# A hybrid encoder layer on one core: turned tiles by way of DRAM, a bound on close short products, and new planner estimates

## The chip, the cores and the metric

The kernel runs on one core of one Trainium2 chip. The metric is the time of one execution in device microseconds (us), given as the median of several runs. The kernel before takes 1050.35 us (median of three runs, 1049.75 to 1050.82).

The core has five engines that run on their own and meet at semaphores: TensorE (PE in the profile, with its weight loads as PEld), VectorE (DVE), ScalarE (ACT), GpSimd (POOL) and SyncE (SP), which here does nothing but issue transfers.

## The reference

One layer over 512 frames of width 2048, all in float32. A wide projection gives the inputs of two mixers that both read the same x; their gated outputs are joined and projected back.

```python
proj = jnp.einsum('btd,dc->btc', h, w_in[l])              # 512 x 2048 by 2048 x 8320
rw = _token_shift(proj[..., :RWKV_COLS], shift_mu[l])
hg = proj[..., RWKV_COLS:]
o_rwkv, v_first = _rwkv7_branch(rw, ...)                  # 16 heads of 64
o_hgrn = _hgrn2_branch(hg, lower_bounds[l], g_norm_w[l])  # 8 heads of 128
y = jnp.einsum('btc,cd->btd', jnp.concatenate([o_rwkv, o_hgrn], -1), w_out[l])
h = _layer_norm(ALPHA * h + y, ln_w[l], ln_b[l])
```

The first mixer steps a 64 x 64 state for each head through time:

```python
sa = jnp.einsum('bhij,bhj->bhi', S, a_t)
S = S * w_t[:, :, None, :] + sa[..., None] * b_t[:, :, None, :] + v_t[..., None] * k_t[:, :, None, :]
out = jnp.einsum('bhij,bhj->bhi', S, r_t)
```

The second is a gated linear recurrence with a decay for each channel, in its chunkwise form.

## The kernel before, in words

**The large products.** Each float32 operand is split into a high and a low part of a faster type (`split`: one ACT copy, `wh`, and one DVE subtraction, `wl`), and three products of 128 x 128 by 512 columns stand for one exact product (`three`, line 457; in the first units line 1205). There are 65 column units of 128 in the input projection and 16 row and column blocks in the output projection, each with 16 steps over the inner dimension. Weights arrive as 512 KB tiles `wr`.

**The mixers are fed in between.** Both mixers are written as Python generators that yield single operations, and a planner (class `Plan`) places them between the large products while the program is written. It keeps a clock for each engine, advances it by an estimated cost for each operation, and after every large product it asks the threads (`pump`, `step`): an operation is put into its engine's instruction stream if by these clocks its inputs are there about now, else its thread waits. `LEAD`, `SLACK` and `EARLY` say how near is near enough. The hardware then runs each engine's stream strictly in order, and semaphores, not the planner, hold an instruction back. A wrong estimate changes no result, but it puts an instruction where it waits, with everything behind it on its engine.

**Short products.** The mixers need many products of blocks smaller than 128 x 128: mode `"narrow"`, all written by `mm` (line 329). They come in series, which the planner holds until about all of a series can run: 32 by 16 or 32 columns (`blocks32`), 32 x 32 inverses (`quarters` of `rwkv_invert`), 64 x 64 blocks (`folded`, `outputs`), 64 x 128 scores (`rwkv_prep`). A float32 product of this kind is two matmul records and two weight loads in the profile.

**Turned tiles.** Three tiles are needed transposed over all 128 partitions: `bk` (eight times, 512 KB), the values `z` (eight times, 256 KB) and the keys of six of the heads of the second mixer (192 KB). `turned` (line 402) does it in two steps: one DVE instruction transposes every 32 x 32 block in place (`dtr`), and then transfers from SBUF to SBUF put the blocks where they belong, 16 for `bk` and the keys and 8 for `z`, each 32 partitions by pieces of 128 bytes. The profile shows them as `q<-q`, `zz<-ksq` and `g<-ksq`, all issued by line 310 (`send`).

**Groups.** Heads go through in pairs: `rwkv_prep` makes operands and scores and then turns; `rwkv_invert` inverts; `folded` forms the products for the scan; `rwkv_scan` steps over the chunks; `outputs`, `rwkv_finish`; and for the other mixer `hgrn_heads` and `hgrn_out`. The reciprocal square roots of the norms are computed on POOL (`rsqrt`, line 384), and a DVE instruction multiplies by them.

**Buffers.** PSUM has four banks for large products (`main`) and four for the rest (`mix`). A `main` bank is emptied by `shift`, `gates` or `silu2` on ACT and DVE (lines 342, 343, 361). The split weight parts `wh`, `wl` have three buffers each.

Of the kernel before, what the change touches and what calls it, by code (L numbers as in the profile page):

```python
# [15 lines left out]
P = 128  # L16
T = 512
# [45 lines left out]
class Plan:  # L63
# [9 lines left out]
             ("whole", "narrow"): 0.1, ("narrow", "main"): 0.26, ("narrow", "whole"): 0.2}  # L73
    REST = 1.5
    LEAD = -0.35
    SLACK = 0.6
    EARLY = 0.5

    def __init__(self, room):
# [4 lines left out]
        self.ready, self.busy, self.banks = {}, {}, set()  # L84
        self.room = room
# [69 lines left out]
    def add(self, queue, gen):  # L155
        queue.append([gen, None, False])
# [4 lines left out]
    def step(self, th):  # L161

        now = self.clock["pe"]
        gen, item, held = th
        if not held:
# [4 lines left out]
            th[1:] = item, True  # L170
        if callable(item):
            if not item():
                return False
        else:
            way = self.best(item)
            end, s, r, e, f = way
            if e == "pe":
                if r > now + self.LEAD or not self.worth(item, now):
# [3 lines left out]
            self.issue(item, way)  # L182
        th[2] = False
# [58 lines left out]
def mixer_kernel(ctx, tc, head, x_r, w_all, par, up, ln_wb, consts, hmask, out):  # L242
# [53 lines left out]
    def landed(*tiles):  # L296
# [8 lines left out]

        return test
# [13 lines left out]
    def mm(o, l, r, start=True, stop=True, **kw):  # L320
# [61 lines left out]
    def rsqrt(o, i):  # L382
        return Op([("pool", 0.25 + size(o) * 0.19,
                    lambda: pool.tensor_tensor(o, i, mhalf[:, : size(o)], ALU.pow))], [i], [o])

    def memset(o, v):
        return Op([("pool", 0.1, lambda: pool.memset(o, v))], [], [o])
# [9 lines left out]
    def turned(dst, src, tmp, rows=4, base=0):  # L397


        name = dst.tensor.name  # L400
# [36 lines left out]
    whole_parts = set()  # L437

    def ready(i, home=None):

        if i < 2 * nload and i not in parts:
            parts[i] = home() if home else tuple(st(t, [P, QT], F32R) for t in ("wh", "wl"))

# [8 lines left out]
    def three(ps, lh, ll, rh, rl, first, last):  # L452
        n = size(rh)
        for i, (l, r) in enumerate(((lh, rh), (lh, rl), (ll, rh))):
            plan.clock["pe"] += n / 2400 + 0.0135 + plan.turn("main")
# [11 lines left out]
    def part(i, width):  # L467

        ready(i)
        hi, lo = parts[i]  # L470
# [155 lines left out]
    hc = [slice(64 * h, 64 * h + 64) for h in range(2)]  # L626

    def rwkv_prep(S, p):
# [75 lines left out]
        S["ar"], S["bk"] = ar, bk  # L704
# [39 lines left out]
        z = take("zz", [P, NCH, P])  # L744
        yield room(ksq=1)
        tmp = take("ksq")
        yield from turned(z, chunks(v), chunks(tmp), rows=2, base=64)
# [3 lines left out]
    def folded(SS, sc):  # L751
# [4 lines left out]
        yield landed(*zs, *bks, sc)  # L756
        pvs = [take("main") for _ in SS]
        pbs = [take("mix") for _ in SS]
        for half, (z, bk, pv, pb) in enumerate(zip(zs, bks, pvs, pbs)):
            for c in range(NCH):  # L760
                i, cs = half * 16 + 2 * c, slice(c * C, c * C + C)
                for h in range(2):
                    yield mm(pv[hc[h], cs], sc[64:128, 0, i + h], z[64:128, c, hc[h]])
                    yield mm(pb[hc[1 - h], cs], sc[0:64, 0, i + 1 - h], bk[0:64, c, hc[1 - h]])
        more = plan.free("mix", 2)
# [10 lines left out]
        if more:  # L776
            yield from beside()
# [902 lines left out]
```

## Time and profile before

| | |
|---|---|
| median of three runs | 1050.35 us (1049.75 to 1050.82) |
| the profiled execution's own time | 1049.71 us |
| its span, first to last instruction | 1047.9 us |
| granted TensorE clock, mean | 0.999 |
| PE busy | 1034.7 us (99%), 7708 matmul records |
| PEld busy | 857.5 us (82%) |
| DVE / ACT / POOL busy | 754.5 (72%) / 436.8 (42%) / 41.8 us (4%) |
| share of the 16 DMA engines | 37.1%, in 97 824 packets, most of them (67 120) under 512 bytes |

The span is cut off at the first and last instruction, so the execution's own time is 1.8 us longer than it. Ends of matmuls are modelled: a large product is shown as 393 ns long while the next one starts about 227 ns after it, so distances between starts say more than durations. In views of waits, "issue" is time in which the engine waited for nothing that the profile shows. In a timeline a row holds equal instructions that follow each other; its second number runs from the start of the first to the end of the last.

### The profile page before, as it was taken

The numbers are of one execution on the slowest core, as the hardware profiler recorded it, in microseconds if no ns is written. First come the engines' busy times: TensorE is split into PE (matmuls) and PEld (weight loads), VectorE is DVE, ScalarE is ACT, GpSimd is POOL, SyncE is SP. The second block draws the span as 40 slices with busy tenths as digits, with TensorE's granted clock in tenths as the row PEclk, the third lists the DMA queues.
The fourth block names the chain that finished last, engine by engine and source line by source line (L and its number), as shares of the span: only waits on it lengthen the run. The fifth ranks groups of instructions, "written<-read, shape, count | busy, mean of one in ns | idle before, by whom it ended". The sixth has DMA issues, their size and how long they took to land.

```text
span 1047.9 us, 19640 instructions
## 1 busy us (share of the span) xinstructions
PE 1034.7 (99%) x7708; PEld 857.5 (82%) x7708; DVE 754.5 (72%) x1599; ACT 436.8 (42%) x817; POOL 41.8 (4%) x77
## 2 busy tenths in 40 slices
PE   9999999999999999999999999999999999999997
PEld 7888888888888888878888788888888888888885
DVE  7474898767759988667689767775999886526456
ACT  6444434543443355353533364435335444223321
POOL 0000001001000010010000100100001011000000
PEclk9999999999999999999999999999999999999999
DMA  9135342133253432224443222344342245445613
GB/s 332 53 103 130 90 104 85 60 93 99 77 140 94 123 87 68 87 74 113 112 116 104 82 73 73 105 110 106 105 117 81 64 157 183 145 129 170 193 60 131
DMA packets 98061, 116.03 MB, mean 111 GB/s; under 512 B 67120, under 2 KB 68912, under 8 KB 97840
## 3 DMA queue, kind: packets, MB, share of 16 engines
q1 hardware_dynamic: 97824, 114.57, 37.1%
q8 instruction: 61, 1.00, 0.4%
q14 instruction: 32, 0.26, 0.1%
q10 hardware_dynamic: 144, 0.20, 0.1%
HBM read 99.92 MB, written 7.34 MB: 102 GB/s over the span
## 4 chain that ended last, share of the span: by engine, by line
PE 93%; DMA 2%; DVE 2%; SPq 1%; issue 1%; ACT 0%; POOL 0%; DVEq 0%
PE main L457 70%; PE mix L329 11%; PE mix L457 8%; PE main L1205 3%; DMA wr<-w_all 2%; PE main L329 1%; PE mix L333 1%; SPq L310 1%; DMA q<-head 0%; DVE t L352 0%; DVE wl L352 0%; DVE inv L361 0%; DMA g<-ksq 0%; ACT t L342 0%; DVE q L361 0%
## 5 line engine op out<-in xcount | busy, mean ns | idle before, releaser
L457 PE MATMUL main<-xh,wh 128*128 128x512 f32 x864 | 339.6, 393 | 1.9 <-DVE t L361 1.9
L457 PE MATMUL main<-xh,wl 128*128 128x512 f32 x864 | 341.2, 395 | 0.0
L457 PE MATMUL main<-xl,wh 128*128 128x512 f32 x864 | 339.7, 393 | 0.0
L342 ACT ACTIVATE wh<-wr 128x512 fp32r<-128x512 f32 x299 | 186.5, 627 | 244.7 <-PE main L457 193.6
L352 DVE TENSOR_TENSOR wl<-wr,wh 128x512 fp32r<-128x512 f32 x299 | 203.3, 682 | 75.1 <-ACT wh L342 73.6
L457 PEld LDWEIGHTS main<-xh,wh 128*128 128x128 f32 x864 | 162.4, 188 | 35.3 <-DVE t L361 2.3
L457 PEld LDWEIGHTS main<-xh,wl 128*128 128x128 f32 x864 | 162.4, 188 | 33.3 <-DVE wl L352 0.3
L457 PEld LDWEIGHTS main<-xl,wh 128*128 128x128 f32 x864 | 162.3, 188 | 33.2
L457 PE MATMUL main<-wl,xh 128*128 128x512 f32 (+1 forms) x262 | 102.2, 390 | 0.3 <-DVE wl L352 0.3
L457 PE MATMUL main<-wh,xh 128*128 128x512 f32 (+1 forms) x262 | 102.1, 390 | 0.0
L457 PE MATMUL main<-wh,xl 128*128 128x512 f32 (+1 forms) x262 | 101.8, 388 | 0.0
L457 PEld LDWEIGHTS main<-wl,xh 128*128 128x128 f32 x262 | 49.2, 188 | 10.3 <-DVE wl L352 0.6
L457 PEld LDWEIGHTS main<-wh,xh 128*128 128x128 f32 x262 | 49.2, 188 | 10.2 <-ACT wh L342 0.2
L457 PEld LDWEIGHTS main<-wh,xl 128*128 128x128 f32 x262 | 49.2, 188 | 9.8
L361 DVE SCALAR_TENSOR_TENSOR bd<-mix,pc,bd 64x64 f32<-64x64 f32 x112 | 31.7, 283 | 17.1 <-PE mix L329 15.0
L343 ACT ACTIVATE t<-main,om 128x512 f32<-128x512 f32 x33 | 22.2, 686 | 51.6 <-PE main L457 42.4
L342 ACT ACTIVATE t<-mix 64x128 f32<-64x128 f32 (+2 forms) x65 | 17.6, 272 | 56.6 <-PE mix L329 28.2
L352 DVE TENSOR_TENSOR inv<-inv 64x30 f32<-64x30 f32 (+14 forms) x120 | 38.5, 321 | 2.8
L352 DVE TENSOR_TENSOR inv<-inv,inv 64x30 f32<-64x30 f32 (+14 forms) x120 | 38.5, 321 | 2.7
L361 DVE SCALAR_TENSOR_TENSOR t<-main,pr,t 128x511 f32<-128x511 f32 x33 | 24.3, 745 | 19.7 <-ACT t L343 19.6
L352 DVE TENSOR_TENSOR t<-t,tot 128x256 f32<-128x256 f32 x96 | 37.5, 417 | 0.3
L343 ACT ACTIVATE t<-main 128x512 f32<-128x512 f32 x32 | 18.6, 595 | 32.5 <-PE main L457 32.3
(218 smaller groups left out, 1311.9 us busy)
## 6 DMA issues: line engine op xcount, KB each, us to landing
wr<-w_all SPq DMA_DIRECT2D x156, 512.0 KB, 3.7
q<-head SPq DMA_DIRECT2D x15, 448.0 KB, 6.1
q<-q SPq DMA_DIRECT2D x128, 32.0 KB, 2.7
g<-x_r SPq DMA_DIRECT2D x16, 256.0 KB, 4.0
spill<-g SPq DMA_DIRECT2D x12, 256.0 KB, 3.7
t<-spill SPq DMA_DIRECT2D x12, 256.0 KB, 4.3
out<-q SPq DMA_DIRECT2D x12, 256.0 KB, 2.5
zz<-ksq SPq DMA_DIRECT2D x64, 32.0 KB, 3.0
```

The costliest lines, as they stand in the source:

```text
L310: nc.sync.dma_start(o, i)
L329: return Op([("pe", cost, lambda: pe.matmul(o, l, r, start=start, stop=stop, **kw))], [l, r], [o], mode="narrow" if narrow else "main" if ...
L333: return Op([("pe", 0.11, lambda: pe.transpose(o, i, ident))], [i], [o])
L342: return "act", cost, lambda: sc_e.activation(o, i, f, scale=scale)
L343: return "act", cost, lambda: sc_e.activation(o, i, f, scale=scale, bias=bias)
L352: return dve_op([a, b], o, lambda: dve.tensor_tensor(o, a, b, f), base=0.16 if o.shape[0] < P and size(o) == C and o.tensor.name in tags e ...
L361: return dve_op([a, b], o, lambda: dve.scalar_tensor_tensor(o, a, s, b, f1, f2), per=0.00113, base=0.085 if o.shape[0] == P else 0.25 if s ...
L457: pe.matmul(ps, l, r, start=first and i == 0, stop=last and i == 2)
L1205: pe.matmul(pss[a], *ops, start=k == 0 and low == of == 0, stop=k == KT - 1 and low == 1)
```

## The change

There are three parts. Besides these, `z` is laid out in another order of its columns (four blocks of 32 first, then chunks), with the reads of it adapted.

**1. Turned tiles.** `turned` writes the tile, after the same 32 x 32 transposes, to a DRAM scratch tile `far` in one transfer, waits in the planner until its estimate says that it has landed, and loads it back in one transfer for each block of 32 rows (four for `bk` and the keys, two for `z`), in pieces of 1 KB (384 bytes for the keys). The order of blocks inside a partition is then not the one that the products need for `bk` and the keys, so one copy on ACT puts it right. The turning of `bk` and `z` becomes a thread of its own (`rwkv_turn`), so the preparation of the next head need not stand behind it.

**2. A bound.** A series of short products is started only if those of the last 3.0 us and the new ones together are at most 68 (`BURST`, `WITHIN`, `room_for`); each series says its length by `batch`. In `folded` the third series is always held apart.

**3. Estimates.** Costs of short products, of the way back from them, of `rsqrt` and `memset` on POOL and of the large products are new; transfers of turned tiles are taken as landed 4.0 us after their issue (2.6 before); and the planner now knows when the buffers `wh` and `wl` come free.

```diff
@@ class Plan
-             ("whole", "narrow"): 0.1, ("narrow", "main"): 0.26, ("narrow", "whole"): 0.2}
+             ("whole", "narrow"): 0.1, ("narrow", "main"): 0.11, ("narrow", "whole"): 0.1}
...
+    BURST, WITHIN = 68, 3.0
...
             if op.mode == "narrow":
                 self.rest = end + self.REST
+                self.short.append(end)
...
+    def room_for(self, n):
+
+        since = self.clock["pe"] - self.WITHIN
+        while self.short and self.short[0] < since:
+            self.short.pop(0)
+        return not self.short or len(self.short) + n <= self.BURST
...
@@ def step
         if callable(item):
             if not item():
                 return False
+            th[3] = getattr(item, "batch", th[3])
         else:
...
             if e == "pe":
+                if th[3] and item.mode == "narrow":
+                    if not self.room_for(th[3]):
+                        return False
...
+            if item.mode == "narrow":
+                th[3] = 0
@@ def mm
-        if r.dtype == F32R:
-            cost = n / 2400 + 0.0135
+        if cost:
+            pass
+        elif r.dtype == F32R:
+            cost = n / 2400 + 0.0145
         elif narrow:
-            cost = 0.025 if m <= 32 else 0.06 if m <= 64 else 0.16
+            cost = 0.0135 + n * 0.0002 if m <= 32 else 0.06 if m <= 64 else 0.115
@@ def rsqrt
-        return Op([("pool", 0.25 + size(o) * 0.19,
+        return Op([("pool", {1: 0.5, 4: 1.35, 8: 1.8}[size(o)],
@@ def turned
-        yield dtr(tmp, src)
+        far = dpool.tile([P, rows, size(tmp) // rows], F32, tag=nm("far"), name=nm("far"))
+        yield dtr(tmp.rearrange("p b c j -> p c b j"), src)
         yield lambda: by_now(tmp)
-        for a in range(4):
-            for b in range(rows):
-                yield lambda: plan.clock["sp"] <= plan.clock["pe"] + 0.2
-                o = base + 32 * b
-                send(dst[o : o + 32, :, 32 * a : 32 * a + 32],
-                     tmp[32 * a : 32 * a + 32, :, 32 * b : 32 * b + 32], 0.65)
-        plan.ready[name] = plan.busy[tmp.tensor.name] = (plan.clock["sp"] + 2.6, "dma")
+        yield lambda: plan.clock["sp"] <= plan.clock["pe"] + 0.2
+        send(far, tmp.rearrange("p b c j -> p b (c j)"))
+        there = plan.busy[tmp.tensor.name] = (plan.clock["sp"] + 4.0, "dma")
+        for b in range(rows):
+            yield lambda: there[0] <= plan.clock["pe"] and plan.clock["sp"] <= plan.clock["pe"] + 0.2
+            send(dst(b).rearrange("i a c j -> i a (c j)"), far[:, b].rearrange("(a i) x -> i a x", a=4))
+        plan.ready[dst(0).tensor.name] = (plan.clock["sp"] + 4.0, "dma")
@@ def ready, def part
+                ring.append(i)
+                before = ring[-1 - BUFS["wh"]] if len(ring) > BUFS["wh"] else -1
+                for t in parts[i]:
+                    plan.busy[t.tensor.name] = (over.get(before, 0.0), "pe")
...
+        for k in range(len(over), min(i, last_parts)):
+            over[k] = plan.clock["pe"]
@@ def rwkv_prep
-        yield landed(bk, ar)
-        yield room(mix=2, main=3)
-        pss = [take(tag) for tag in ("main", "mix") for h in range(2)]
+        yield landed(bk, ar, n=16)
+        yield lambda: plan.free("mix", 2) and plan.free("main", 3) or plan.free("mix", 4)
+        pss = [take(tag) for tag in ("main" if plan.free("main", 3) else "mix", "mix") for h in range(2)]
...
+        plan.add(turns, rwkv_turn(S, bk, r))
+
+    def rwkv_turn(S, bk, r):
         yield room(q4=1)
         tmp = take("q4", [P, NCH, P])
-        yield from turned(bk, bk, tmp)
-        drop(tmp)
+        bk4 = blocks(bk.rearrange("p c f -> p (c f)"), NCH)
+        yield from turned(lambda b: bk4[32 * b : 32 * b + 32], bk, blocks(tmp.rearrange("p c f -> p (c f)"), NCH))
+        yield act(tmp.rearrange("p c (a j) -> p c a j", j=32), bk4.rearrange("p a c j -> p c a j"), AF.Copy)
+        drop(bk)
+        S["bk"] = tmp
@@ def folded
-        yield landed(*zs, *bks, sc)
+        yield landed(*zs, *bks, sc, n=64)
...
-        if not more:
-            yield room(mix=2)
-            yield landed(sc)
-            yield from beside()
+        yield room(mix=2)
+        yield landed(sc, n=32)
+        yield from beside()
@@ def hgrn_out
-            yield from turned(kt, tiles(k)[:, 0:3], tiles(tmp)[:, 0:3])
+            g4 = blocks(g[:, : 3 * P], 3)
+            yield from turned(lambda b: g4[32 * b : 32 * b + 32], kt, blocks(tmp[:, : 3 * P], 3))
             drop(tmp)
+            yield act(kt.rearrange("p c (a j) -> p c a j", j=32), g4.rearrange("p a c j -> p c a j"), AF.Copy)
```

**How the instruction streams move.** The number of products on PE is the same. The first place is the first series of 64 x 64 products on PE (`folded`, for the first pair of heads). `mix` tiles with sources `t` belong to `hgrn_heads`, `zz` and `q` with `big` to `folded`; `main` with `xh`, `wh`, `wl` are large products. Before, 64 products of one and 64 of the other stand in one series:

```order
L457 MATMUL main_1850<-xl_85,wh_1654 128x512
L329 MATMUL mix_1847<-t_1049 32x16 x16
L329 MATMUL mix_1847<-t_1258 32x16 x16
L329 MATMUL mix_1847<-t_954,t_1050 32x16 x16
L329 MATMUL mix_1847<-t_1161,t_1259 32x16 x16
L329 MATMUL main_1924<-zz_872,big_694 64x64
L329 MATMUL mix_1926<-q_447,big_694 64x64
...
L329 MATMUL mix_1927<-q_933,big_694 64x64
L457 MATMUL main_1850<-xh_69,wl_1655 128x512
```

In the change the same products stand in two series, with many large products and another short series between them:

```order
L485 MATMUL main_1285<-wh_1679,xh_80 128x512
L348 MATMUL mix_1736<-t_1075 32x16 x16
L348 MATMUL mix_1736<-t_1272 32x16 x16
L348 MATMUL mix_1736<-t_961,t_1076 32x16 x16
L348 MATMUL mix_1736<-t_1173,t_1273 32x16 x16
L485 MATMUL main_1285<-wl_1680,xh_80 128x512
...
L485 MATMUL main_1955<-xh_69,wh_1884 128x512
L348 MATMUL main_1936<-zz_1000,big_694 64x64
L348 MATMUL mix_1938<-q_743,big_694 64x64
```

Over the whole stream there were 36 such unbroken series, and there are now 43; the longest was 128 products (five more had 96) and is now 64.

The second place is SP at the first turn of `bk` (`q_447`; `wr` are weights). Before:

```order
L310 DMA wr_751<-w_all 128x1024
L310 DMA q_447<-q_735 32x8x32 x6
L310 DMA wr_792<-w_all 128x1024
L310 DMA q_447<-q_735 32x8x32 x8
L310 DMA wr_834<-w_all 128x1024
L310 DMA q_447<-q_735 32x8x32 x2
L310 DMA wr_885<-w_all 128x1024
```

and in the change:

```order
L327 DMA wr_764<-w_all 128x1024
L327 DMA far_744<-q_743 128x1024
L327 DMA up_789<-up 128x256
L327 DMA q_447<-far_744 32x4x256
L327 DMA wr_813<-w_all 128x1024
L327 DMA q_447<-far_744 32x4x256 x3
L327 DMA wr_855<-w_all 128x1024
```

SP's transfers in all go from 530 to 336. The third place is DVE in `hgrn_out` of the third head, where `rs` holds the factors of a norm that POOL computes between the `TENSOR_SCALAR` and the product with `mix`, and the instruction after that product frees a `main` bank. Before:

```order
L365 TENSOR_REDUCE rs_4837<-t_3389 128x4
L358 TENSOR_SCALAR rs_4837<-rs_4837 128x4
L352 TENSOR_TENSOR wl_4846<-wr_4703,wh_4845 128x512
L352 TENSOR_TENSOR t_3389<-mix_4825,rs_4837 128x512
L361 SCALAR_TENSOR_TENSOR t_4859<-main_4212,pr,t_4859 128x511
```

and in the change, where other work has moved in before the `TENSOR_SCALAR`, while one `wl` still stands behind it:

```order
L384 TENSOR_REDUCE rs_4688<-t_3368 128x4
L371 TENSOR_TENSOR wl_4696<-wr_4545,wh_4695 128x512
L371 TENSOR_TENSOR t_3105<-t_3105,sm_4619 128x512
L377 TENSOR_SCALAR rs_4688<-rs_4688 128x4
L371 TENSOR_TENSOR wl_4718<-wr_4640,wh_4717 128x512
L371 TENSOR_TENSOR t_3368<-mix_4675,rs_4688 128x512
L380 SCALAR_TENSOR_TENSOR t_4725<-main_4173,pr,t_4725 128x511
```

More of the change, by code (lines that the diff above doesn't have):

```diff
@@ L84, in __init__ @@
         self.ready, self.busy, self.banks = {}, {}, set()
+        self.short = []
         self.room = room
@@ L155, in add @@
     def add(self, queue, gen):
-        queue.append([gen, None, False])
+        queue.append([gen, None, False, 0])
     def free(self, tag, n=1):
@@ L163, in step @@
         now = self.clock["pe"]
-        gen, item, held = th
+        gen, item, held = th[:3]
         if not held:
@@ L169, in step @@
                 return True
-            th[1:] = item, True
+            th[1:3] = item, True
         if callable(item):
@@ L294, in has, with landed @@
         return lambda: all(n in S for n in names)
-    def landed(*tiles):
+    def landed(*tiles, n=0):
         names = [getattr(t, "tensor", t).name for t in tiles]
@@ L318, in size, with mm @@
         return n
-    def mm(o, l, r, start=True, stop=True, **kw):
+    def mm(o, l, r, start=True, stop=True, cost=None, **kw):
         m, n = size(l), size(r)
         narrow = m < P or l.shape[0] < P
-        if r.dtype == F32R:
-            cost = n / 2400 + 0.0135
+        if cost:
+            pass
+        elif r.dtype == F32R:
+            cost = n / 2400 + 0.0145
         elif narrow:
-            cost = 0.025 if m <= 32 else 0.06 if m <= 64 else 0.16
+            cost = 0.0135 + n * 0.0002 if m <= 32 else 0.06 if m <= 64 else 0.115
         else:
@@ L395, in copy, with blocks, turned @@
         return Op([act_way(o, i, AF.Copy, scale), ("dve", 0.075 + size(o) * 0.00105 + moved(o, i), f)], [i], [o])
-    def turned(dst, src, tmp, rows=4, base=0):
-        name = dst.tensor.name
-        yield dtr(tmp, src)
-        yield lambda: by_now(tmp)
-        for a in range(4):
-            for b in range(rows):
-                yield lambda: plan.clock["sp"] <= plan.clock["pe"] + 0.2
-                o = base + 32 * b
-                send(dst[o : o + 32, :, 32 * a : 32 * a + 32],
-                     tmp[32 * a : 32 * a + 32, :, 32 * b : 32 * b + 32], 0.65)
-        plan.ready[name] = plan.busy[tmp.tensor.name] = (plan.clock["sp"] + 2.6, "dma")
+    def blocks(t, n):
+        return t.rearrange("p (a c j) -> p a c j", a=4, c=n)
+    def turned(dst, src, tmp, rows=4):
+        far = dpool.tile([P, rows, size(tmp) // rows], F32, tag=nm("far"), name=nm("far"))
+        yield dtr(tmp.rearrange("p b c j -> p c b j"), src)
+        yield lambda: by_now(tmp)
+        yield lambda: plan.clock["sp"] <= plan.clock["pe"] + 0.2
[5 more added lines that the diff above has]
+        plan.ready[dst(0).tensor.name] = (plan.clock["sp"] + 4.0, "dma")
     splits = plan.queue()
@@ L435, in load @@
             plan.fetched(raws[j], 4 * HALF)
-    whole_parts = set()
+    last_parts = 2 * nload - 2 * KT
+    whole_parts, over, ring = set(), {}, []
     def ready(i, home=None):
@@ L454, in three @@
         for i, (l, r) in enumerate(((lh, rh), (lh, rl), (ll, rh))):
-            plan.clock["pe"] += n / 2400 + 0.0135 + plan.turn("main")
+            plan.clock["pe"] += n / 2400 + 0.0145 + plan.turn("main")
             plan.mode = "main"
@@ L626, in mixer_kernel, with halves @@
     hc = [slice(64 * h, 64 * h + 64) for h in range(2)]
+    hb = [slice(2 * h, 2 * h + 2) for h in range(2)]
+    def halves(t):
+        return t.rearrange("p (c a j) -> p c a j", a=2, j=32)
     def rwkv_prep(S, p):
@@ L743, in rwkv_prep @@
         yield room(zz=1)
-        z = take("zz", [P, NCH, P])
+        z = take("zz", [P, 4, NCH, 32])
         yield room(ksq=1)
-        tmp = take("ksq")
-        yield from turned(z, chunks(v), chunks(tmp), rows=2, base=64)
+        tmp = take("ksq", [P, 2, NCH, 32])
+        yield from turned(lambda b: z[64 + 32 * b : 96 + 32 * b], chunks(v), tmp, rows=2)
         drop(v, tmp)
@@ L762, in folded @@
                 for h in range(2):
-                    yield mm(pv[hc[h], cs], sc[64:128, 0, i + h], z[64:128, c, hc[h]])
-                    yield mm(pb[hc[1 - h], cs], sc[0:64, 0, i + 1 - h], bk[0:64, c, hc[1 - h]])
-        more = plan.free("mix", 2)
+                    yield mm(pv[hc[h], cs], sc[64:128, 0, i + h], z[64:128, hb[h], c], cost=0.036)
+                    yield mm(pb[hc[1 - h], cs], sc[0:64, 0, i + 1 - h], bk[0:64, c, hc[1 - h]], cost=0.036)
         prs = []
@@ L780, in folded @@
                 yield copy(bk[0:64, :, hc[h]], chunks(pb[hc[h]]))
-                yield copy(z[0:64, :, hc[h]], chunks(pv[hc[h]]), scale=-1.0)
+                yield copy(z[0:64, hb[h]].rearrange("p a c j -> p c a j"), halves(pv[hc[h]]), scale=-1.0)
             drop(pv, pb)
-        if not more:
-            yield room(mix=2)
-            yield landed(sc)
-            yield from beside()
+        yield room(mix=2)
+        yield landed(sc, n=32)
+        yield from beside()
         def keep():
@@ L801, in outputs @@
             z = S["zz"]
-            yield lambda z=z: by_now(z)
+            test = lambda z=z: by_now(z)
+            test.batch = 32 - 16 * half
+            yield test
             for c in range(0, NCH, 2):
@@ L806, in outputs @@
                         yield mm(po[hc[e], c // 2 * P + 64 * h : c // 2 * P + 64 * h + 64],
-                                 sc[:, 1, half * 16 + 2 * (c + e) + h], z[:, c + e, hc[h]])
+                                 sc[:, 1, half * 16 + 2 * (c + e) + h], z[:, hb[h], c + e])
         for S, po in zip(SS, pss):
@@ L834, in quarters @@
         def quarters(prod, *needs):
-            yield landed(*needs)
+            yield landed(*needs, n=32)
             pt = take("mix")
@@ L871, in rwkv_scan @@
             more = c < NCH - 1
-            zs = [zz[:, c] for zz in zzs]
+            zs = [zz[:, :, c] for zz in zzs]
             news = [bds[c % 2] for bds in bdss]
@@ L1067, in hgrn_out @@
         g = take("g")
-        kt, state = tiles(g)[:, 0:3], tiles(k)[:, 0:3]
+        kt = state = tiles(k)[:, 0:3]
         if h < 6:
@@ L1145, in mixer_kernel @@
     scans = [plan.queue(), plan.queue()]
-    groups, finishes, preps = plan.queue(), [plan.queue(), plan.queue()], plan.queue()
+    groups, finishes, preps, turns = plan.queue(), [plan.queue(), plan.queue()], plan.queue(), plan.queue()
     heads, stores = plan.queue(), plan.queue()
```

17 lines of the change are left out of this document (9 added, 8 removed).

## The prediction

> **What bounds the kernel now.** I read the page first, then the waits of PE, then PE's timeline around each wait.
>
> ```profile
> span 1047.9 us, 19640 instructions
> PE 1034.7 (99%) x7708; PEld 857.5 (82%) x7708; DVE 754.5 (72%) x1599; ACT 436.8 (42%) x817; POOL 41.8 (4%) x77
> PE 93%; DMA 2%; DVE 2%; SPq 1%; issue 1%; ACT 0%; POOL 0%; DVEq 0%
> ```
>
> PE is busy from end to end, and the change leaves its products as they are. So only two things can move the time: stretches in which PE has nothing to do, and the cost of going from large to short products and back. The waits of PE (us in total, times, longest) say how much the first can give:
>
> ```profile
> PE main L457 <- DVE t L361: 1.9, 1, 1.9
> PE mix L329 <- ACT ksq L1422: 1.5, 1, 1.5
> PE mix L329 <- issue: 1.3, 3, 0.8
> PE main L329 <- issue: 1.3, 1, 1.3
> PE mix L329 <- DMA g<-ksq: 0.6, 1, 0.6
> ```
>
> Some 6.6 us in seven waits, of which the second (1.5 us) is the layer norm at the end, which the change does not touch. The other five microseconds, somewhat more by the distances between starts, are all that could be won; each item is worked out below.
>
> **The bound on short products: what it takes away.** The four waits on "issue" lie inside series of short products, and no semaphore ends them. On the weight-load side of PE (start, length, then in brackets the idle time):
>
> ```profile
> 187.67 0.13 PEld L329 LDWEIGHTS main<-zz,big 64*64 64x64 f32 x1 [1.42 <-issue]
> 391.85 0.25 PEld L329 LDWEIGHTS mix<-big 64*64 64x64 f32 x6 [0.90 <-issue]
> 592.93 0.46 PEld L329 LDWEIGHTS mix<-t 128*32 128x32 f32 x43 [0.47 <-issue]
> 601.57 0.15 PEld L329 LDWEIGHTS mix<-t,t 128*32 128x32 f32 x6 [0.31 <-issue]
> ```
>
> They add up to 3.10 us. What PE waits for is, I think, its own instructions. The transfers of the whole run and of 184.9 to 186.5 us have a queue for them:
>
> ```profile
> q8 instruction: 61, 1.00, 0.4%
> q8 instruction: 1, 0.02, 4.8%
> ```
>
> 61 blocks carry 1.00 MB, 16 KB each, and PE's 2 x 7708 = 15 416 records divided by 61 are 253 a block. A short product is two loads and two matmuls, so a block holds 63 of them. The second row is one such block, just before the wait that ends at 187.67. Two series of the same 96 products show the loss by windows (the length stands before the comma, PE's busy time and records behind it):
>
> ```profile
> 386.80:392.70 5.90, 5.13 (x195) 4.77 (x195) 5.40 (x13) 3.86 (x7) 0.00 (x0) 1.00 0.33 92
> 608.90:613.80 4.90, 4.90 (x195) 4.58 (x195) 4.61 (x11) 4.48 (x9) 0.00 (x0) 1.00 0.36 110
> ```
>
> The first needs 1.0 us more for the same 195 records. The second shows that a long series need not wait: it depends on where in it the block ends. In the change no series is over 64 products and each is followed by large ones, which take 0.23 us for two instructions, so two block ends no longer fall into one series. I take 3.0 of the 3.10 us. Bounds: 3.1, and 2.0 if some of the thirteen series of 64 still wait as the one before 601.57 did (0.31).
>
> The Trainium skill speaks against it: "Runtime: NRT & Kernel Launch", section "Instruction fetch mechanics", says that instructions come in blocks of 256 and that fetching is hidden because dispatch is slower than the fill. The block size agrees with 253; hidden it is not, by the 1.42 us. By that rule this term would be nothing, which is the second rival.
>
> **What the bound costs.** Seven more series (43 instead of 36). What one costs beside its products, from PE's timeline and its groups:
>
> ```profile
> 178.56 0.39 PE L457 MATMUL main<-wl,xh 128*128 128x512 f32 x1
> 178.79 0.39 PE L457 MATMUL main<-wh,xl 128*128 128x512 f32 x1
> 179.11 0.78 PE L329 MATMUL mix<-inv,inv 32*32 32x32 f32 x64
> 179.81 0.50 PE L457 MATMUL main<-wh,xh 128*128 128x512 f32 x1
> 180.15 0.39 PE L457 MATMUL main<-wl,xh 128*128 128x512 f32 x1
> ...
> L329 PE MATMUL mix<-inv,inv 32*32 32x32 f32 x256 | 3.0, 194 | 0.0
> ```
>
> From 178.79 to 180.15 are 1.36 us. Two large products take 2 x 0.23 (178.56 to 178.79). The 64 records go at (0.78 - 0.19)/63 = 9.4 ns each, since the last one alone lasts 0.194: 0.60. Left over are 0.30 us for the way there and back. Seven times that is 2.1 us; I take 2.2, a little more, since other shapes may turn more slowly. Bounds: 1.4 (only the visible 0.09 and 0.11 at the two turns) and 2.6.
>
> **The estimate for POOL.** The longest wait, at 460 us, in the timelines of ACT, DVE, POOL and PE:
>
> ```profile
> 456.57 0.68 ACT L343 ACTIVATE t<-main,om 128x512 f32<-128x512 f32 x1
> 456.91 0.17 DVE L358 TENSOR_SCALAR rs<-rs 128x4 f32<-128x4 f32 x1
> 457.16 1.39 POOL L384 TENSOR_TENSOR rs<-rs,mhalf 128x4 f32<-128x4 f32 x1 [3.81 <-DVE rs L358]
> 458.58 0.69 DVE L352 TENSOR_TENSOR t<-mix,rs 128x512 f32<-128x512 f32 x1 [0.90 <-POOL rs L384]
> 459.19 0.74 DVE L361 SCALAR_TENSOR_TENSOR t<-main,pr,t 128x511 f32<-128x511 f32 x1
> 457.68 0.39 PE L457 MATMUL main<-xh,wl 128*128 128x512 f32 x1
> 459.98 0.50 PE L457 MATMUL main<-xh,wh 128*128 128x512 f32 x1 [1.92 <-DVE t L361]
> ```
>
> PE lacks a `main` bank. The DVE instruction that frees it could have begun at 457.7, behind `wl`; it stands behind the multiplication by `rs`, for which POOL needs 1.39 us where the old estimate said 0.25 + 4 x 0.19 = 1.01. With 1.35 in the table the multiplication is written 0.34 us later, and other DVE work moves ahead, as the third place of the order shows. PE loses 459.98 - 457.68 - 0.23 = 2.07 us; I take 2.0 as won. Bounds: 2.07, and nothing, since one `wl` (0.7 us) still covers only half of POOL's time there.
>
> **The turned tiles.** Before, one of their transfers came late once, and PE stood before the product that reads it:
>
> ```profile
> 257.39 0.39 PE L457 MATMUL main<-xl,wh 128*128 128x512 f32 x1
> 258.33 0.91 PE L329 MATMUL mix<-ia,g 128*128 128x128 f32 x6 [0.56 <-DMA g<-ksq]
> ```
>
> That is 0.94 - 0.23 = 0.7 us, and I take 0.7 as won (bounds 0 and 0.7), because the planner now allows 4.0 us in place of 2.6. The new way has no row; its neighbours, first two issues of the first turn, then sizes with the median from issue to landing, and the spread over `spill`:
>
> ```profile
> 75.21 4.02 SPq L310 DMA_DIRECT2D q<-q  x6
> 85.76 1.24 SPq L310 DMA_DIRECT2D q<-q  x2
> ...
> wr<-w_all SPq DMA_DIRECT2D x156, 512.0 KB, 3.7
> q<-q SPq DMA_DIRECT2D x128, 32.0 KB, 2.7
> spill<-g SPq DMA_DIRECT2D x12, 256.0 KB, 3.7
> up<-up SPq DMA_DIRECT2D x8, 128.0 KB, 3.4
> ...
> DMA to landing us min/median/max: 2.0/4.2/6.2
> ```
>
> Before, sixteen issues ran from 75.2 to 87.0, and with 2.7 for the last a turn took 14.5 us. Now: a store of 512 KB, of the size of `wr` and the direction of `spill`, which I put at 4.2 (3.7 to 6.2); four issues of some 0.45; a load of 128 KB, like `up`, 3.4. That is 9.4 us. The planner allows 4.0 + 0.44 for each of the two ways, so neither should be late on the median. New is a copy on ACT:
>
> ```profile
> L342 ACT ACTIVATE wh<-wr 128x512 fp32r<-128x512 f32 x299 | 186.5, 627 | 244.7 <-PE main L457 193.6 <-PE mix L457 32.9 <-DMA wr<-w_all 6.9
> ```
>
> For 1024 columns twice 0.627, 1.25 us, eight times, and 384 columns (0.5) six times: 13 us on an engine that is busy for 42%. These hide behind ACT's waits for PE, 244.7 us before 299 weight copies, 0.8 us before each. If a load lands late, the copy stands at the head of ACT, and the weight copies (`wh`) behind it are late once 0.8 us is used up; then PE waits. I add 0.6 us for such waits and others that the new order brings (bounds 0 and 4: four of fourteen copies late by 1 us beyond the cover). Estimates of large products and the buffers `wh` and `wl` move instructions but remove none; they are in that term.
>
> **The sum.** -3.0 + 2.2 - 2.0 - 0.7 + 0.6 = -2.9 us on a span of 1047.9. The profiled execution took 1049.71, 1.8 more than its span, and the median of the runs, 1050.35, is 0.6 above it; both stay. 1050.35 - 2.9 gives 1047.4.
>
> **Rivals.** (1) The round trip comes late; this one is slower. For it: it is two waits for a landing in series, and `spill` rows reach 6.2 us. The Trainium skill ("DMA: Bandwidth & Descriptors", "Why small descriptors are slow (HBM only)") adds that transfers within SBUF do not suffer from small pieces, so larger ones would win little. The trace does not decide that: 2.7 us for 32 KB of 128-byte pieces stand beside 3.4 for 128 KB. Against the rival: the medians above. It decides once store and load together pass 4.44 + 4.44 + 0.8 = 9.7 us. With 6.2 and 5.0 a copy is 1.5 us beyond that; in five of the fourteen it costs 7.5 us: 1054.9.
> (2) The waits on "issue" are no matter of series length, or come back elsewhere, while the seven series are paid: 1047.4 + 3.0 = 1050.4. For it: the wait at 601.57 fell in a series of only 64 products. Against it: the two windows.
> (3) The bank is late as before, because POOL still takes 1.39: 1047.4 + 2.0 = 1049.4. For it: the one `wl`.
> (4) All goes to the good side: turns at 1.4, no new waits, nothing left on "issue": 1047.4 - 0.8 - 0.6 - 0.1 = 1045.9. For it: the planner's costs of the turns are nearer to the rows than before. Against it: an order that moves everywhere rarely brings no wait.
>
> **How the numbers follow.** Forecast 0.50 (1046.0 to 1048.6), rival 1 0.12, rival 2 0.14, rival 3 0.14, rival 4 0.10. A measurement tells 0.2%, 2.1 us, from no change: faster is below 1048.2. That takes most of the forecast (0.46), rival 4 and some of rival 3 (0.03): 0.59. Slower, above 1052.5, is rival 1 (0.11) with a little of rival 2: 0.13. The same has the rest, 0.28. The range leaves out the far side of rivals 1 and 4: 1044.8 to 1051.8.
>
> **What would show it.** Right: no wait on "issue" above 0.4 us within a series; no wait of a `main` product for `DVE t` near 460 us; `far` stores landing in 3.7 to 4.8 us and loads under 4; PE waits without the end under 2 us. Wrong: PE waiting for ACT `wh` behind a copy that waits for `far` (rival 1), waits on "issue" as long as before (rival 2), or turns to short products that cost much more than 0.30 us each.

## The result, and the profile after

The changed kernel takes 1044.37 us (median of four runs, 1044.08 to 1045.53), the kernel before 1050.59 in the same session (four runs, 1049.75 to 1051.51). The ratio is 0.9943, with a 95% interval of 0.9925 to 0.9960: 6 us faster. The forecast was 1047.4, in a range of 1044.8 to 1051.8. The direction was right; the gain is about twice the forecast, and the time lies 0.4 us below the range.

The page of the changed kernel (span, busy times, chain):

```profile
span 1042.3 us, 19372 instructions
PE 1033.4 (99%) x7708; PEld 854.4 (82%) x7708; DVE 760.9 (73%) x1614; ACT 439.0 (42%) x816; POOL 42.4 (4%) x77
PE 94%; DVE 2%; ACT 1%; DMA 1%; issue 1%; SPq 0%; DVEq 0%; ACTq 0%
```

PE still sets the time, with the same 7708 records, and the span is 5.6 us shorter (1047.9 to 1042.3). The profiled execution took 1044.08, 1.8 more than its span, as before. All waits of PE that the view lists (total, times, longest):

```profile
PE mix L348 <- ACT ksq L1461: 1.5, 1, 1.5
PE mix L1194 <- DVE inv L1192: 1.1, 1, 1.1
PE mix L348 <- DVE ksq L371: 0.5, 1, 0.5
PE mix L348 <- DVE t L371: 0.4, 1, 0.4
PE main L1244 <- ACT xh L361: 0.4, 1, 0.4
PE main L485 <- ACT t L362: 0.2, 1, 0.2
```

The four waits on "issue", the 1.9 us for a `main` bank, the late `g` and a small wait for `wl` are gone; the last one (0.3 in the view) stands in the view of before but not in the prediction's list. The first two rows, the end and the start of the program, are as before. The last four are new.

By the distances between the starts of PE's products, the 5.6 us come apart like this. "Forecast" is the term of the prediction; a minus is time won:

| item | forecast | measured |
|---|---|---|
| waits on "issue" in short series | -3.0 | -3.2 |
| seven more series | +2.2 | +0.9 |
| bank wait at 460 us | -2.0 | -2.1 |
| late `g` at 258 us | -0.7 | -0.7 |
| waits of the new order, less the old `wl` wait | +0.6 | +1.7 |
| 64 x 64 series, beyond their waits on "issue" | none | -2.5 |
| sum | -2.9 | -5.9 (0.3 not assigned) |

The measured numbers are sums over all starts, from one profiled execution of each kernel. For the waits, the usual distance of such a pair is taken off. For the series, it is what ways in, ways out and changes of shape inside a series cost beyond the products: 9.75 us before (36 series, 9 changes of shape), 10.60 after (43 and 5). For the last item, the distances within runs of 64 x 64 products fell from 19.9 to 15.0 us, of which 2.4 are waits on "issue" and stand in the first item.

The new transfers, from the view of transfers (KB, median us from issue to landing):

```profile
far<-q SPq DMA_DIRECT2D x8, 512.0 KB, 5.1
q<-far SPq DMA_DIRECT2D x32, 128.0 KB, 3.6
```

The loads are near where they were put (3.4), the stores later than the 4.2 taken. One of them cost a little. In ACT's timeline the copy behind a load stands at the head for 1.90 us, and two rows later ACT empties a `main` bank:

```profile
132.94 1.06 ACT L361 ACTIVATE q<-q 128x1024 f32<-128x1024 f32 x1 [1.90 <-DMA q<-far]
133.91 0.61 ACT L361 ACTIVATE ksq<-t 128x512 fp32r<-128x512 f32 x1
134.43 1.06 ACT L362 ACTIVATE t<-main 128x512 f32<-128x512 f32 x2
```

PE misses that bank at 135.5 us (`main` for ACT `t`, 0.35 us between the starts). This is the first rival's mechanism, once and small.

### The profile page after: what moved, and what is told of

It is laid out like the page before. It is cut to its first block, busy times and chain, and to the rows that moved or that the text cites. A ratio compares the mean times of both kernels' runs of the same rounds, so it can differ in the third digit from the quotient of the medians.

```text
span 1042.3 us, 19372 instructions
## 1 busy us (share of the span) xinstructions
PE 1033.4 (99%) x7708; PEld 854.4 (82%) x7708; DVE 760.9 (73%) x1614; ACT 439.0 (42%) x816; POOL 42.4 (4%) x77
## 4 chain that ended last, share of the span: by engine, by line
PE 94%; DVE 2%; ACT 1%; DMA 1%; issue 1%; SPq 0%; DVEq 0%; ACTq 0%
PE main L485 71%; PE mix L348 10%; PE mix L485 8%; PE main L1244 3%; PE main L348 1%; PE mix L352 1%; DVE wl L371 1%; DMA q<-head 0%; DMA q<-far 0%; DVE inv L380 0%; DVE inv L371 0%; DVE t L371 0%; ACT L362 0%; DVE big L390 0%; ACT t L362 0%
## 5 line engine op out<-in xcount | busy, mean ns | idle before, releaser
L361 ACT ACTIVATE t<-mix 64x128 f32<-64x128 f32 (+3 forms) x60 | 16.8, 280 | 53.7 <-DVE zz L371 25.6
```

Source lines behind the costliest of these rows:

```text
L361: return "act", cost, lambda: sc_e.activation(o, i, f, scale=scale)
```

## The experiments

Ratios are to the kernel before, run beside each on the same chip. The twelve runs come in three groups of four kernels, and the kernel before had medians of 1049.58, 1049.43 and 1048.76 us in them. "Issue" is the sum of PE's waits on "issue" in the profile.

| kernel | series, longest | issue | span | time | ratio (95%) |
|---|---|---|---|---|---|
| bound alone | 41, 64 | none | 1042.0 | 1043.77 | 0.9929 (0.9906 to 0.9952) |
| bound alone, again | 41, 64 | none | 1041.8 | 1043.02 | 0.9947 (0.9934 to 0.9959) |
| whole change, again | 43, 64 | none | 1042.3 | 1044.86 | 0.9963 (0.9949 to 0.9978) |
| transfers and bound | 42, 64 | none | 1044.2 | 1046.03 | 0.9969 (0.9958 to 0.9980) |
| transfers alone | 38, 96 | 4.6 | 1052.4 | 1054.19 | 1.0047 (1.0033 to 1.0060) |
| estimates alone | 37, 160 | 4.7 | 1052.1 | 1054.06 | 1.0049 (1.0036 to 1.0062) |
| `rsqrt` estimate alone | 38, 128 | 3.8 | 1050.6 | 1052.27 | 1.0031 (1.0015 to 1.0048) |

### The bound alone

This is the kernel before with `room_for` and the lengths given to it; transfers and estimates are as before.

```diff
+    BURST, WITHIN = 68, 3.0
...
-        yield landed(*zs, *bks, sc)
+        yield landed(*zs, *bks, sc, n=64)
```

> The kernel before with the bound alone (BURST, WITHIN, the lengths of the series, and the third series of folded held apart); old transfers, old estimates. 41 series in place of 36, the longest 64. Theory F (PE waits for instruction blocks when a long short series uses one up): waits on issue inside a series fall from 3.1 us to under 0.5, five more turns cost 5 x 0.30 = 1.5, so 1.1 us faster, 1049.4, if the other waits stay. Rival (length has nothing to do with it): the waits stay, 1.5 us slower, 1052.

It came out 5.9 us shorter in span, 0.9929. PE's waits:

```profile
PE mix L345 <- ACT ksq L1436: 1.5, 1, 1.5
PE mix L1169 <- DVE inv L1167: 1.1, 1, 1.1
PE main L1219 <- ACT xh L358: 0.9, 1, 0.9
```

Between start and end of the program nothing is left: no "issue", and also no bank wait and no late `g`, though neither POOL's estimate nor the transfers were touched. Both theories put this kernel 5 us or more too high. So two terms of the prediction had the right size and the wrong cause.

### Is it the place of a block's end? The same order, moved by 64 instructions

Sixteen products of 32 x 32, which are 64 PE instructions, are added to the warm-up products, whose results nobody reads. The order of everything behind them stays. This is done once on the kernel before and once on the changed one.

```diff
     for _ in range(WARM):
         pe.matmul(warm, zero, zero)
+    for _ in range(16):
+        pe.matmul(warm[:32, :32], zero[:32, :32], zero[:32, :32])
```

> The kernel before with 16 more warm-up products of 32 x 32 at the very start (0.3 us, 64 instructions); every other instruction in the same order. Theory F with blocks of 256 instructions: all block ends move 64 instructions earlier in the program, so the waits on issue move to other places: that at 187.7 us stays long (about 2), that near 592 grows from 0.5 to about 2.9 and that at 601.6 goes; in sum 3.1 becomes about 6 us and the kernel some 3 us slower, 1053 to 1054. Rival (the waits belong to the products or their data): same places, same 3.1 us, 1050.8.

> The changed kernel with the same 16 warm-up products at the start. Theory F: with no series over 64 no position of the block ends makes PE wait, so no wait on issue inside a series and the time stays, 0.2 to 0.4 us above the changed kernel. Rival (the changed kernel is free of such waits only by its present alignment): waits of 0.3 to 1.5 us come up, 1045 to 1047.

The kernel before went to 1056.55 us, ratio 1.0069 (1.0046 to 1.0092), some 3 us more than theory F said; the execution that was profiled has the lowest of its ten times, 1053.54. Its waits moved, on the weight-load side:

```profile
187.60 0.19 PEld L329 LDWEIGHTS mix<-q,big 64*64 64x64 f32 x2 [1.64 <-issue]
411.78 0.14 PEld L329 LDWEIGHTS mix<-t,t 128*32 128x32 f32 x2 [1.09 <-issue]
595.87 0.29 PEld L329 LDWEIGHTS mix<-t,t 128*32 128x32 f32 x11 [2.40 <-issue]
```

Before they stood at 187.67, 391.85, 592.93 and 601.57, 3.10 us in all; now there are three, 5.13 us, two of them in places that had none or a shorter one, with no other instruction in another order. The changed kernel with the same sixteen products has no such wait, as theory F said, but took 1046.01 us, 0.9963 (0.9949 to 0.9978), 1.6 us more than in the first measurement where 0.2 to 0.4 were expected. The profiled execution, which has the highest of its nine times (1047.66), is 3.6 us longer in span than that of the changed kernel, and 3.2 of these lie in its first 12 us, where the added products and the first large ones ran slowly. Whether that holds for the median too is not shown.

The place can be counted. With PE's records numbered from 0 in order of time, semaphore instructions included, the first record behind every wait on "issue" stands at a number that leaves 193 when divided by 256: all 4 of the kernel before, all 3 here, 4 with the transfers alone, 5 with the estimates alone, 4 with the `rsqrt` estimate alone, and the 3 of the two variants below. That is 23 of 23. The prediction's 253 a block left out the semaphore instructions; with them the kernel before has 15 609 records in its 61 blocks, 256 each.

The blocks' own transfers are in the traces too. For the longest wait above, the view of the queues from 593.3 to 594.5 us has one block, whose transfer ends at 594.37:

```profile
q8 instruction: 1, 0.02, 4.8%
```

PE goes on at 595.87, 1.5 us behind it. With transfers and block ends paired in order, all 23 waits end 1.1 to 1.6 us behind the end of such a transfer, and at the other 812 block ends of the fourteen traces, which PE passes without such a wait, no transfer ended less than 1.2 us earlier. So a block's end is where PE waits, the late block is what it waits for, and a long series is what makes the end come too early. The Trainium skill ("Runtime: NRT & Kernel Launch", "Instruction fetch mechanics") has the block of 256 right and calls crossing it mostly hidden; the 2.40 us above are not.

### Turned tiles: what many small transfers cost in the 64 x 64 series

This is the changed kernel with `z` loaded in eight pieces in place of two. The order on PE, DVE, ACT and POOL is the same, and 37 semaphore waits in place of 13 stand in PE's instruction stream ahead of 64 x 64 products.

```diff
+            if rows == 2:
+                for a in range(4):
+                    send(dst(b)[:, a].rearrange("i c j -> i (c j)"), far[32 * a : 32 * a + 32, b], 0.11)
+                continue
```

> The changed kernel, but z comes back from DRAM in eight loads of 32 KB in place of two of 128 KB. The order on PE, DVE, ACT and POOL is the same; PE has 24 more waits for landings ahead of 64 x 64 products (37 in place of 13, counted in the instruction stream). Theory S (the 3 us that the prediction missed are waits for many small transfers: each costs PE about 77 ns in a short series, the gaps of the series at 386.8 us before): the four folded series of 64 products go from 2.34 to about 2.8 us each and the kernel gets 1.8 us slower, about 1046.2. Rival L (it is the new layout of z that made the folded series faster): no change, within 0.3 us.

It took 1045.94 us, ratio 0.9958 (0.9939 to 0.9977), with a span of 1043.9. The first series of 64 products, by the last large product ahead of it and the first one behind it, in the changed kernel:

```profile
186.18 0.39 PE L485 MATMUL main<-xh,wh 128*128 128x512 f32 x1
...
188.53 0.50 PE L485 MATMUL main<-xl,wh 128*128 128x512 f32 x1
```

with eight loads:

```profile
187.11 0.39 PE L489 MATMUL main<-xh,wh 128*128 128x512 f32 x1
...
189.69 0.50 PE L489 MATMUL main<-xl,wh 128*128 128x512 f32 x1
```

and with the bound alone, where `z` and `bk` still come in 8 and 16 transfers and 45 such waits are in the stream:

```profile
191.87 0.39 PE L473 MATMUL main<-xl,wh 128*128 128x512 f32 x1
...
194.72 0.50 PE L473 MATMUL main<-xh,wl 128*128 128x512 f32 x1
```

These are 2.35, 2.58 and 2.85 us for the same 64 products, and no row in them waits for a transfer: the tiles are there, and the passing of the semaphores is what takes the time. All four series took 9.4, 10.4 and 11.4 us. Twenty-four more waits cost 1.0 us, 43 ns each on the mean. The theory was right in kind and had put them at 77. The starts show it directly: within the 64 x 64 series two matmul records follow each other after 0.02 us, and where a semaphore instruction lies between them in time after 0.04 (12 places in the changed kernel), 0.05 (24 with eight loads) or 0.08 (29 with the bound alone). The rest of this kernel's 1.6 us of span is not the loads' price in these series: its wait at 136 us grew from 0.35 to 0.91 between the starts, 0.4 us were lost in the first 12 us, and 0.4 were won back later.

### Each part without the bound, and without the estimates

These are four kernels: transfers alone, estimates alone, the one POOL estimate alone, and transfers with the bound but old estimates. The POOL estimate is this line:

```diff
-        return Op([("pool", 0.25 + size(o) * 0.19,
+        return Op([("pool", {1: 0.5, 4: 1.35, 8: 1.8}[size(o)],
```

> The first part of the change alone: turned tiles by way of DRAM; no bound, old estimates. 38 series, the longest 96 products. Theory F (PE's instructions arrive in blocks of 256, and a series that is too long for the gap waits) leaves up to 3 us of waits on issue, wherever a block ends late in a series of 96; S wins 2.4 in the 64 x 64 series and the late DMA (0.7) is gone; two more series cost 0.6: a span of 1045.4 with the issue waits as before, 1042.4 without any. Rival (the transfers do nothing, the bound is the whole change): 1047.5 to 1048.5.

It is slower than before, and its span of 1052.4 us lies above what theory F and the rival expected. Its waits are

```profile
PE mix L348 <- issue: 3.3, 3, 1.6
PE main L483 <- DVE t L380: 2.9, 1, 2.9
PE main L483 <- issue: 1.3, 1, 1.3
```

with one more loss behind them. After 1.57 us without work the large products run at half their pace:

```profile
191.33 0.45 PE L348 MATMUL mix<-big 64*64 64x64 f32 x8 [1.57 <-issue]
...
192.52 0.40 PE L483 MATMUL main<-xh,wh 128*128 128x512 f32 x1
192.76 0.48 PE L483 MATMUL main<-xl,wh 128*128 128x512 f32 x1
193.03 0.63 PE L483 MATMUL main<-xh,wl 128*128 128x512 f32 x1
193.46 0.63 PE L483 MATMUL main<-xh,wh 128*128 128x512 f32 x1
...
196.64 0.39 PE L483 MATMUL main<-xh,wh 128*128 128x512 f32 x1
```

The starts lie 0.24 us apart at first, then 0.43; by 196.64 the pace is the usual one again. Three waits of this kernel have such a stretch behind them.

> The third part alone: the new estimates of short and large products, of the ways back, of POOL and of the buffers wh and wl, on the kernel before; transfers and series rules as before. 37 series, the longest 160 products. Theory F expects waits on issue of at least the 3.1 us of before, since a series of 160 is 640 instructions, more than two blocks. The prediction's third term expects no 2 us wait for a main bank near 460, so a span of 1046 to 1047 with the issue waits as before, 1048 or more with longer ones. Rival (better estimates shorten the run by themselves): under 1045.

This one is also slower, as theory F allowed (1048 or more). The bank wait near 460, which the estimates were to take away, is longer than ever:

```profile
PE main L465 <- DVE t L363: 3.4, 1, 3.4
PE mix L331 <- issue: 2.9, 4, 1.4
PE main L465 <- issue: 1.8, 1, 1.8
```

> One estimate alone on the kernel before: the reciprocal square root on POOL, 1.35 in place of 1.01 for four columns. The prediction: the 2 us wait of a main product for DVE t near 460 us is gone, the waits on issue (3.1) stay, two more series cost 0.6: a span of 1046.5. Rival O (the wait went because the order changed at all, since the bound alone removed it too without this estimate): the wait stays or another of its size stands elsewhere, a span of 1047.5 to 1049.

The bank wait went as predicted, and the sum did not follow (a span of 1050.6 us, above both expectations): the waits on "issue" grew to 3.8, and a transfer of the keys is now late twice.

```profile
PE mix L329 <- DMA g<-ksq: 2.2, 2, 1.7
PE main L329 <- issue: 2.0, 2, 1.6
PE mix L329 <- issue: 1.8, 2, 1.6
```

> The change without its third part: turned tiles by way of DRAM and the bound, with the planner's old estimates of products, turns, POOL and buffers. 42 series, none over 64. Beside the kernel with the bound alone (span 1042.0) only the transfers differ. Theory S (the many small transfers cost time in the 64 x 64 series, because each is a semaphore of its own that PE passes ahead of a product that is as short as the passing): the four series of 128 records take 2.34 each in place of 2.73 to 2.96, 2.0 in all; one more series +0.3; the span 1040.3, plus up to 1.5 for waits of a new order. Rival L (the shorter series of the whole change came from its order, not from the transfers): they stay at 2.7 to 2.9, and the span is 1042 to 1043.5.

It is faster than before and slower than the bound alone, and its span of 1044.2 us lies above both expectations. The four series took 2.34 us each, as theory S said (9.4 in place of 11.4), so the transfers do win 2 us there. But this order has waits of its own, some 3 us between starts, more than they win:

```profile
PE mix L352 <- DVE t L371: 0.8, 1, 0.8
PE main L483 <- ACT wh L361: 0.7, 2, 0.5
PE main L483 <- DVE wl L371: 0.3, 1, 0.3
PE mix L348 <- DVE ksq L371: 0.3, 1, 0.3
```

Taken together: with the bound, 1043 to 1046 us; without it, 1052 to 1054 for each of the other parts, against 1049 for the kernel before. The bank wait stands in the kernel before, with transfers alone and with estimates alone, and in none of the other kernels of the table; the POOL estimate is neither needed nor enough to lose it.

### The bound alone beside the whole change, and two margins

> The bound alone once more, beside the whole change on the same chip. Theory: the whole change is not faster than its second part; by the profiled spans (1042.0 and 1042.3) they lie within 0.1%. Rival (the first look had a fast chip, and transfers and estimates are worth 1 to 2 us): this one is 0.1 to 0.2% slower than the whole change.

> The whole change once more, beside its second part alone: a ratio of 0.994 to the kernel before, as first measured, and within 0.1% of the bound alone.

The bound alone took 1043.02 us (five runs, 1042.58 to 1043.67) against 1044.86 (five runs, 1044.11 to 1045.47) for the whole change: the two ranges do not meet, and the second part alone is 1.8 us faster than the whole. The theory had the sign, not the size; the rival had the sign the other way. The profiled spans, 1041.8 and 1042.3, are only 0.5 apart.

Two variants of the whole change, each with one number changed:

```diff
-    LEAD = -0.35
+    LEAD = -0.5
```

> The whole change with LEAD -0.5 in place of -0.35: an operation of PE is placed only when its inputs have been there for half a microsecond by the planner's clocks. Four waits of the changed kernel come from inputs that were placed as ready and were not: 0.35 at 135.5 (ACT t), 0.55 at 164 (DVE t in a series), 0.63 and 0.13 at 496 and 530 (DVE ksq), 1.7 us in all; no series is longer than before, and there are 41 of them in place of 43. Theory M (what is left to win are small waits of the order): span 1040.6 to 1041.8 against 1042.3. Rival O (each order brings waits of its own, whatever the margin): 1042 to 1044.

```diff
-    BURST, WITHIN = 68, 3.0
+    BURST, WITHIN = 68, 3.5
```

> The whole change with the bound's window 3.5 us in place of 3.0 (WITHIN). Series stay at 64 products or less, so theory F expects no wait on issue either way; 42 series, 0.3 less. The order changes after the first mixers; by the order the wait at 496 should be gone (0.63) and the one at 135.5 stay: 1041.4. Rival O: 1042 to 1044.

They took 1044.20 us (0.9957, 0.9944 to 0.9970; span 1041.6) and 1044.74 us (0.9960, 0.9946 to 0.9973; span 1042.0). Neither can be told from the whole change (0.9963) nor beats the bound alone, though the first span lies where theory M put it. The second is not the 1041.4 that was expected. With `LEAD` at -0.5 the waits at 135.5 and 164 us are gone and the one at 496 has shrunk from 0.63 to 0.36 us between the starts, but this row is new:

```profile
PE mix L348 <- issue: 0.9, 2, 0.7
```

Both series in which it waits are no longer than 64 products, and their block ends are at 193 again. The other variant has one such wait of 0.2. So the bound makes these waits rare and short; it does not exclude them.

## Why the prediction was right or wrong

**The waits on "issue".** This term was right in size (3.2 us for 3.0) and in cause, as the shift by 64 instructions, the count of 193 and the landing of the blocks show. That rival 2 would put them elsewhere is refuted for this kernel; but with the very same bound and another margin some of it (0.9 us) comes back, the lower bound given to this term.

**Seven more series.** This term was too dear: 0.9 us where 2.2 were taken and 1.4 was the lower bound. The 0.30 us were measured on a series of one shape and multiplied by seven. Several of the new series come from cutting one that held two shapes, and a change of shape inside a series costs some 0.12 us of its own (1.11 us for 9), which is saved by the cut. That saving was not in the term.

**The bank wait at 460 us.** This was the right number from a wrong step, which is luck. The step said that with 1.35 in the table the multiplication by `rs` is written later and other DVE work moves ahead. Here is the same chain in the changed kernel, on DVE, POOL and PE:

```profile
444.44 0.16 DVE L377 TENSOR_SCALAR rs<-rs 128x4 f32<-128x4 f32 x1
444.58 0.69 DVE L371 TENSOR_TENSOR wl<-wr,wh 128x512 fp32r<-128x512 f32 x1
444.69 1.45 POOL L403 TENSOR_TENSOR rs<-rs,mhalf 128x4 f32<-128x4 f32 x1 [1.92 <-DVE rs L377]
446.17 0.69 DVE L371 TENSOR_TENSOR t<-mix,rs 128x512 f32<-128x512 f32 x1 [0.90 <-POOL rs L403]
446.78 0.74 DVE L380 SCALAR_TENSOR_TENSOR t<-main,pr,t 128x511 f32<-128x511 f32 x1
446.62 0.39 PE L485 MATMUL main<-xh,wh 128*128 128x512 f32 x1
446.85 0.39 PE L485 MATMUL main<-xl,wh 128*128 128x512 f32 x1
```

It is instruction for instruction the chain of before, with the same 0.90 us on DVE behind POOL. Nothing in it was repaired; PE has a bank and goes on (446.62, 446.85). What differs is where in a unit of 48 products PE stands when the chain runs, and that moves with every order. Rival 3 named the chain rightly (POOL still too slow for one `wl` to cover) and was wrong that PE must then wait.

**The late `g`.** The 0.7 us are won, but the 4.0 us that the planner now allows did not win them: with the bound alone, and 2.6 us allowed, they are gone too, and with the `rsqrt` estimate alone they are 2.2 us. In the kernel before with the sixteen added products, whose order is the same, they are gone as well. So this is luck too: what decides is when PE gets there.

**Waits of the new order.** This term was mis-sized: 2.2 us between starts in place of 0.6, of which 0.5 are given back by the old `wl` wait. They stand in four places, at 7.5, 135.5, 164.2 and 495.6 us; one comes from a copy behind a load, 0.35. In the profiles these waits and two more series take away what the transfers win over the second part alone. The 1.8 us between the medians are more than the profiled spans show, and where the rest lies is open.

**The term that was missing.** The 64 x 64 series became 2.5 us shorter beyond their waits on "issue". The prediction began with "only two things can move the time", idle stretches of PE and the ways between large and short products, and so held the pace inside a series for fixed. It counted the transfers' issues on SP and their landing, and not that each landing has a semaphore that PE has to pass; waits that were over long ago were taken as free. At 43 to 61 ns each (1.0 us for the 24 of the eight loads; 2.0 us for 33, since 45 stand there with the bound alone and 12 with transfers and bound) they are free behind a product of 0.23 us (before, the next one starts 0.227 us later on the median with or without a semaphore instruction between) and not in a series where a product takes some 37 ns. Not all of the 2.5 us are the new transfers: with the bound alone, whose transfers are those of before, the distances are 17.0 us, so 0.5 are won without them and 2.0 with them. This step, together with the price of the series, is why the gain was twice the forecast: 2.5 and 1.3 us more than forecast, less 1.1 for the waits of the new order.

**The late round trip.** The first rival did not come true, although the stores were later than taken (5.1 us). Of fourteen copies one is seen to have held PE up.

## What to carry to other kernels

Count the instructions of an engine between its slow stretches: here a run of short products on PE that used up a block of 256 faster than the next one arrived waited at the block's end, and a cap on such runs won more than all three parts together. Part of that was luck: of its 5.9 us of span some 2.8 are the bank wait and the late `g`, which it was not made for. A semaphore that was already satisfied still cost its passing, some 43 ns; in series of products as short as that, fewer and larger transfers won time on PE, not on the queues. And a wait that vanishes when an order changes has not been repaired: try the parts of a change one by one, since here one part alone was faster than all three.

## What the hardware showed that was not expected

After some waits PE runs at half pace. In the kernel before with the sixteen products added, behind the longest of its three waits:

```profile
596.20 0.80 PE L457 MATMUL main<-wh,xh 128*128 128x512 f32 x1
596.79 0.63 PE L457 MATMUL main<-wl,xh 128*128 128x512 f32 x1
597.22 0.63 PE L457 MATMUL main<-wh,xl 128*128 128x512 f32 x1
...
601.48 0.53 PE L457 MATMUL main<-wh,xh 128*128 128x512 f32 x1
601.85 0.40 PE L457 MATMUL main<-wl,xh 128*128 128x512 f32 x1
```

Starts are 0.43 us apart for 5 us, and about 2.4 us are lost (twelve times 0.20), as much as in the wait itself. The granted clock in that stretch is 0.50, the third number from the end of its row:

```profile
594.90:601.60 6.70, 5.74 (x25) 4.55 (x25) 4.83 (x17) 2.08 (x5) 0.00 (x0) 0.50 0.25 81
```

The mean granted clock of that execution is 0.995 where the changed kernel has 1.000. Over all its ten executions it is 0.991 to 0.998, with 0.991 in the longest, 1062.12 us; in all 50 executions on record of kernels with the bound it is 0.999 or 1.000. The shortest wait with such a stretch behind it was 1.55 us, in the kernel with the `rsqrt` estimate alone, where another of 1.56 had none; nor had the 1.92 us of the kernel before. The Trainium skill ("TensorE: Matmul & The Clock Gate", "What's actually happening") tells of half rate after an idle window of about 3.4 us that does not start with the idle time; the pace agrees (427 ns a product in these rows), and that waits of half that length can set it off, but need not, is what the runs add. Which of them do was not settled. It gives a long wait on "issue" a second price, and it is part of why the kernels without the bound are 3 to 5 us slower than before.
